# Weight sums of a Strassen product: two of four made by DMAs that add, all of them turned into additions

## The chip, the cores and the metric

The kernel runs on one core of a Trainium2 chip. A core has five engines with an instruction queue each: TensorE (PE), VectorE (DVE), ScalarE (ACT), GpSimd (POOL) and SyncE (SP), beside 16 DMA engines that all queues share. The metric is the device time of one execution in microseconds (us).

## The reference

One layer of a residual block on x of 512 tokens by 2048 features, in float32. What matters here is the second half, the feed-forward part with a hidden width of 8192:

```
h2 = rmsnorm(x, g_mlp)
u  = relu(h2 @ w_up)          # 2048 x 8192
x  = x + (u * u) @ w_down     # 8192 x 2048
return rmsnorm(x, g_final)
```

Before it come an input projection, two kinds of attention (8 heads each) and the output projection `w_out`.

## The kernel before

**Precision.** Every float32 operand of a matmul is split into a high part (a cast to fp32r on ACT, tiles `wh`, `wx`, `fh`) and a low part (value minus high part on DVE, tiles `wl`, `wx`, `fl`), by `split`, lines 60 and 61. `mm3` makes one product of three matmuls: high x high, high x low, low x high (lines 93 to 95). A matmul with `wl` therefore needs DVE's half, one with `wh` alone only ACT's.

**The first feed-forward product.** It is cut by Strassen's method in Winograd's form: of two 2 x 2 block matrices, seven products instead of eight, each on sums of blocks. The activations' seven forms `F[p]` (p = 1 to 7) are made once by `a_form`. The weights go through in 32 units of 256 columns. A unit has four blocks of 128 rows x 8 x 128 float32 (512 KB each): b11 and b12 in one loaded tile, b21 and b22 in another (`wu`, 1024 KB; five such tiles in the pool `rw`, so two and a half units are held; unit 0's b11 and b12 lie in tiles `wq`). Its seven products have 24 matmuls of 256 columns each, 8 steps of three. They need the weights in this form:

- p = 1: b11 itself; p = 5: b11 replaced by b12 - b11 (line 557)
- p = 6: b11 replaced by b22 - b11 (line 559); p = 2: b21; p = 3: b22
- p = 4: b21 replaced by b21 - b11 (line 561); p = 7: b12 replaced by b22 - b12 (line 563)

The sums are made in place by DVE. Each product takes a pair of tiles for the high and the low part from four pairs that go round in the order in which the program calls the products (`hi_lo`), so a product's split waits until PE has read the product four before it. That order is, for each unit: product 1 of the new unit, 4 of the old one, 5, 6 of the new, 3 of the old, 2 and 7 of the new. The results go to PSUM (`psa`, `psb`, `psc`), from there by ACT and DVE to `c`, and every two units are turned, seven forms at a time, into the left operand of the second product and stored to DRAM (`store_form`, tiles `st`, `ufd`).

**What sets the order.** The program is written in the order of these calls; a scheduler then fixes the order of each engine's instructions before the run, by costs of its own. At run time each queue goes strictly in its order and waits by semaphores.

**The start of this product.** The output projection ends with four additions of its result to x (line 487, DVE), 16 transposes on PE (line 496), the scaling on ACT (line 500) and the last quarter of the forms F. Unit 0's weights are split in the middle of it.

## Time and profile before

| | |
|---|---|
| time, median of 3 runs | 2093.42 us (2093.0 to 2095.84) |
| span of the profiled execution | 2090.6 us |
| own time of the profiled execution | not recorded apart from its span; the median of the runs is 2.8 us above the span |
| PE, DVE, ACT, POOL busy | 99%, 75%, 49%, 3% of the span |
| first feed-forward product | about 802 to 1470 us of the span |
| DMA queue of SP and POOL | 335.64 MB on SP's queue, none on POOL's |

Page and trace are of one execution. The span runs from the first to the last instruction; a busy share is the time an engine's instructions took, and instructions that only issue DMAs are not counted as busy. A row of a group names the line, the engine, the operation, out<-in by the program's names with buffer numbers left out, the count, the busy time in us and the mean in ns, and behind the second bar the idle time of the engine just before these instructions and what ended it. A row of waits gives who waited for whom: us in total, times, longest. A row of a stretch of time gives for each engine the busy us and the count, then the granted clock of PE, the share of the DMA engines in use, and GB/s.

### The profile page before, as it was taken

What the parts mean: (1) busy time and instruction counts of PE and PEld (TensorE: products, weight loads), DVE (VectorE), ACT (ScalarE), POOL (GpSimd) and SP (SyncE); (2) the same over time, 40 slices, a digit from 0 to 9 for tenths busy, and PEclk for the clock granted to TensorE, in tenths of its full rate; (3) what the DMA queues carried; (4) which work ended last, traced back from release to release, by engine and by line L of the source; (5) the groups of instructions that cost most, each with busy time, mean ns of one, the idle gap of its engine ahead of it and who ended that gap; (6) DMA issues with size and microseconds to landing.
All of it is one profiled execution on the core that took longest, in us unless ns stands there. A gap on an engine that the chain in (4) does not pass through costs nothing.

```text
span 2090.6 us, 29838 instructions
## 1 busy us (share of the span) xinstructions
PE 2070.1 (99%) x12084; PEld 1841.0 (88%) x12084; DVE 1570.7 (75%) x1744; ACT 1034.2 (49%) x1396; POOL 52.9 (3%) x76
## 2 busy tenths in 40 slices
PE   9999999999999999999999999999999999999998
PEld 8888888888898888999999999999888888888886
DVE  5454545665677567888888888888798988888886
ACT  6333334444445555556665666666744443333433
POOL 0000000010000000000000000000000000000003
PEclk9999999999999999999999999999999999999999
DMA  6323332323323444466566566567856664663732
GB/s 193 81 87 85 83 89 72 90 75 87 81 81 111 147 145 152 138 206 192 185 219 189 185 205 205 176 201 248 299 201 251 249 225 172 249 250 134 271 111 81
DMA packets 239930, 339.68 MB, mean 162 GB/s; under 512 B 7936, under 2 KB 154416, under 8 KB 233776
## 3 DMA queue, kind: packets, MB, share of 16 engines
q1 hardware_dynamic: 238832, 335.64, 48.9%
q8 instruction: 95, 1.56, 0.3%
q10 hardware_dynamic: 960, 2.13, 0.3%
q14 instruction: 43, 0.35, 0.0%
HBM read 272.20 MB, written 65.54 MB: 162 GB/s over the span
## 4 chain that ended last, share of the span: by engine, by line
PE 98%; DVE 1%; ACT 0%; issue 0%; DMA 0%; SPq 0%; ACTq 0%
PE accd L93 8%; PE accd L94 8%; PE accd L95 8%; PE psa L94 6%; PE psa L93 6%; PE psa L95 6%; PE accq L95 6%; PE accq L94 6%; PE accq L93 6%; PE psc L94 3%; PE psc L95 3%; PE psc L93 3%; PE acco L95 3%; PE acco L94 3%; PE acco L93 3%; PE accv L93 3%
## 5 line engine op out<-in xcount | busy, mean ns | idle before, releaser
L60 ACT CAST wh<-wu 128x1024 fp32r<-128x1024 f32 x164 | 170.9, 1048 | 134.8 <-PE psa L94 55.3
L61 DVE TENSOR_TENSOR wl<-wu,wh 128x1024 fp32r<-128x1024 f32 x164 | 199.4, 1221 | 45.0 <-ACT wh L60 44.7
L94 PE MATMUL psa<-fl,wh 128*128 128x256 f32 x776 | 219.8, 283 | 1.8 <-DVE fl L61 1.8
L93 PE MATMUL psa<-fh,wh 128*128 128x256 f32 x776 | 219.9, 283 | 0.5 <-ACT s L572 0.5
L95 PE MATMUL psa<-fh,wl 128*128 128x256 f32 x776 | 219.7, 283 | 0.0
L61 DVE TENSOR_TENSOR wl<-wraw,wh 128x1024 fp32r<-128x1024 f32 (+2 forms) x133 | 158.7, 1194 | 80.1 <-ACT wh L60 73.8
L60 ACT CAST wh<-wd 128x1024 fp32r<-128x1024 f32 (+1 forms) x136 | 134.6, 999 | 168.6 <-PE accd L95 107.5
L60 ACT CAST wh<-wraw 128x1024 fp32r<-128x1024 f32 (+2 forms) x133 | 135.4, 1019 | 156.5 <-PE accq L94 77.6
L95 PE MATMUL accq<-hH,wl 128*128 128x512 f32 x512 | 200.4, 391 | 0.0
L93 PE MATMUL accq<-hH,wh 128*128 128x512 f32 x512 | 200.1, 391 | 0.0
L94 PE MATMUL accq<-hL,wh 128*128 128x512 f32 x512 | 200.0, 391 | 0.0
L61 DVE TENSOR_TENSOR wl<-wd,wh 128x1024 fp32r<-128x1024 f32 (+1 forms) x136 | 155.5, 1153 | 41.9 <-ACT wh L60 41.4
L93 PE MATMUL accd<-wh,uf 128*128 128x512 f32 x436 | 169.7, 389 | 0.9 <-issue 0.9
L94 PE MATMUL accd<-wl,uf 128*128 128x512 f32 x436 | 169.6, 389 | 0.0
L95 PE MATMUL accd<-wh,uf 128*128 128x512 f32 x436 | 169.6, 389 | 0.0
L94 PEld LDWEIGHTS psa<-fl,wh 128*128 128x128 f32 x776 | 149.0, 192 | 2.2 <-DVE fl L61 2.2
L60 ACT CAST wx<-wd 128x1024 fp32r<-128x1024 f32 (+1 forms) x88 | 87.5, 1000 | 127.3 <-PE accd L95 75.9
L93 PEld LDWEIGHTS psa<-fh,wh 128*128 128x128 f32 x776 | 149.0, 192 | 1.0 <-ACT s L572 0.7
L95 PEld LDWEIGHTS psa<-fh,wl 128*128 128x128 f32 x776 | 149.0, 192 | 0.2 <-DVE wl L61 0.2
L61 DVE TENSOR_TENSOR wx<-wd,wx 128x1024 fp32r<-128x1024 f32 (+1 forms) x88 | 100.7, 1153 | 23.6 <-ACT wx L60 23.2
L94 PEld LDWEIGHTS accq<-hL,wh 128*128 128x128 f32 x512 | 96.2, 188 | 19.5
L95 PEld LDWEIGHTS accq<-hH,wl 128*128 128x128 f32 x512 | 96.1, 188 | 19.3
(300 smaller groups left out, 5491.9 us busy)
## 6 DMA issues: line engine op xcount, KB each, us to landing
wu<-in_w_up_dram SPq DMA_DIRECT2D x63, 1024.0 KB, 6.7
ufd<-st SPq DMA_DIRECT2D x98, 512.0 KB, 6.8
wd<-in_w_down_dram SPq DMA_DIRECT2D x48, 1024.0 KB, 6.1
wraw<-in_w_in_dram SPq DMA_DIRECT2D x84, 512.0 KB, 3.7
uf<-ufd SPq DMA_DIRECT2D x42, 1024.0 KB, 5.9
wraw<-in_w_out_dram SPq DMA_DIRECT2D x32, 512.0 KB, 3.6
wd<-in_w_down_dram SPq DMA_DIRECT2D x16, 768.0 KB, 6.2
uf<-ufd SPq DMA_DIRECT2D x14, 768.0 KB, 5.6
```

The lines of the kernel that those rows point to most:

```text
L60: ins = act.copy(hi, src)
L61: lows[0] = dve.tensor_tensor(lo, src, hi.bitcast(F32), op=ALU.subtract)
L93: pe.matmul(out, sh, mh, start=first, stop=False, skip_group_check=True)
L94: pe.matmul(out, sh, ml, start=False, stop=False, skip_group_check=True)
L95: pe.matmul(out, sl, mh, start=False, stop=last, skip_group_check=True)
```

## The change

The sums for p = 5 and p = 7 are made by DMAs that add their source to what lies at the destination: for p = 5 the block b12 is read a second time from DRAM and added to b11; for p = 7 b22 is added to b12 from on-chip memory to on-chip memory. Each sum is issued on POOL's queue in two halves of 256 KB, in runs of 512 bytes. Since they can only add, the signs change: p = 5 uses b12 + b11, p = 6 b22 + (b12 + b11), p = 4 b21 + b11, p = 7 b22 + b12. The forms of the activations and the last step of the results (`self.c`) take the opposite signs in return. Product 5 no longer reads b12, so b12 stays as loaded until p = 7.

```diff
-    def a_form(p, c, out, s=None):
+    def a_form(p, c, out, s=None, sums=False):
...
-            dve.tensor_tensor(s, a21, a22, op=ALU.add)
+            dve.tensor_tensor(s, a21, a22, op=ALU.subtract if sums else ALU.add)
...
-            dve.tensor_tensor(a12, a12, s, op=ALU.subtract)
+            dve.tensor_tensor(a12, a12, s, op=ALU.add if sums else ALU.subtract)
...
+    def add_dma(out, src):
+        for h in (slice(0, KC // 4), slice(KC // 4, KC // 2)):
+            pool.dma_start(out[:, h, :], src[:, h, :], accum_op=ALU.add)
...
+            self.w12 = rows_[0][:, :, (2 * u + 1) * P:2 * (u + 1) * P]
...
             if p == 5:
-                dve.tensor_tensor(b11, b12, b11, op=ALU.subtract)
+                add_dma(b11, self.w12)
             if p == 6:
-                dve.tensor_tensor(b11, b22, b11, op=ALU.subtract)
+                dve.tensor_tensor(b11, b22, b11, op=ALU.add)
             if p == 4:
-                dve.tensor_tensor(b21, b21, b11, op=ALU.subtract)
+                dve.tensor_tensor(b21, b21, b11, op=ALU.add)
             if p == 7:
-                dve.tensor_tensor(b12, b22, b12, op=ALU.subtract)
+                add_dma(b12, b22)
...
-                dve.tensor_tensor(self.c[:, 1, t2], self.m, self.C, op=ALU.add)
+                dve.tensor_tensor(self.c[:, 1, t2], self.C, self.m, op=ALU.subtract)
...
-                dve.tensor_tensor(self.c[:, 1, t1], self.m6, self.C, op=ALU.add)
+                dve.tensor_tensor(self.c[:, 1, t1], self.C, self.m6, op=ALU.subtract)
```

In the changed kernel the line of the adding DMAs is 533, of the sums for p = 6 and p = 4 it is 564 and 566, and of the evictions (before 578, 580, 584) 583, 585, 589. The scheduler also orders the queues anew.

**DVE at unit 10** (`wu_8904` and `wu_8906` before, `wu_8924` and `wu_8926` now, are its two weight tiles; `wu_8669`, `wu_8671` and `wu_8687`, `wu_8689` those of unit 9; a row of L61 that reads such a tile is the low half of a product's split, a row with `st` or of L458 to L464 belongs to `store_form`). Before, from product 1 of unit 10 to its product 5:

```order
L61 TENSOR_TENSOR wl_8912<-wu_8904,wh_8911 128x1024
L464 TENSOR_TENSOR c_8136<-c_8136 128x2x256
L61 TENSOR_TENSOR st_8941<-c_8136,st_8941 128x512
L584 TENSOR_TENSOR c_8603<-s6_8570,psc_8442 128x256
L557 TENSOR_TENSOR wu_8904<-wu_8904 128x8x128
L61 TENSOR_TENSOR wx_8947<-wu_8671,wx_8947 128x1024
L580 TENSOR_TENSOR c_8603<-s1_8703,psb_8674 128x256
L563 TENSOR_TENSOR wu_8904<-wu_8906,wu_8904 128x8x128
L61 TENSOR_TENSOR wl_8977<-wu_8904,wh_8976 128x1024
```

Now, the same stretch:

```order
L61 TENSOR_TENSOR wl_8932<-wu_8924,wh_8931 128x1024
L585 TENSOR_TENSOR c_8620<-s1_8721,psb_8692 128x256
L61 TENSOR_TENSOR wx_8967<-wu_8689,wx_8967 128x1024
L583 TENSOR_TENSOR c_8620<-psc_8693,s7_8921 128x256
L61 TENSOR_TENSOR wl_8998<-wu_8924,wh_8997 128x1024
```

The sums of lines 557 and 563 are gone, and between the two splits of unit 10 stand only two evictions and a split of unit 9. In unit 9 the scheduler put ten rows of `store_form` and others there.

**POOL.** Before, behind the last select of the attention stand only multiplications at the end of the kernel:

```order
L221 AFFINE_SELECT w_5014<-w_5014 128x3x128
L221 AFFINE_SELECT w_5014<-w_5014 128x128
L782 TENSOR_TENSOR m2_14223<-m2_14223,gf_18072 128x512 x4
L782 TENSOR_TENSOR m3_14281<-m3_14281,gf_18072 128x512 x4
L782 TENSOR_TENSOR m4_14339<-m4_14339,gf_18072 128x512 x2
```

Now 64 pairs of DMAs stand between them, here of units 7 to 10 (`<-in_w_up_dram` is the sum for p = 5, `<-wu` that for p = 7):

```order
L533 DMA wu_8215<-wu_8217 128x4x128 x2
L533 DMA wu_8215<-in_w_up_dram 128x4x128 x2
L533 DMA wu_8452<-wu_8454 128x4x128 x2
L533 DMA wu_8452<-in_w_up_dram 128x4x128 x2
L533 DMA wu_8687<-wu_8689 128x4x128 x2
L533 DMA wu_8924<-wu_8926 128x4x128 x2
L533 DMA wu_8687<-in_w_up_dram 128x4x128 x2
L533 DMA wu_8924<-in_w_up_dram 128x4x128 x2
```

As a rule a unit's p = 7 pair stands ahead of its p = 5 pair; in every fourth unit (5, 9, 13 and so on) the next unit's p = 7 pair stands ahead too.

**DVE at unit 0 and 1.** Before, the rows at the end of the output projection:

```order
L61 TENSOR_TENSOR wl_6657<-wq_6647,wh_6656 128x1024
L557 TENSOR_TENSOR wq_6647<-wq_6648,wq_6647 128x1024
L61 TENSOR_TENSOR wl_6688<-wq_6647,wh_6687 128x1024
L487 TENSOR_TENSOR x2_6212<-x2_6212,acco_6208 128x512
L487 TENSOR_TENSOR x2_6212<-x2_6212,acco_6209 128x512
```

Now:

```order
L61 TENSOR_TENSOR wl_6657<-wq_6647,wh_6656 128x1024
L487 TENSOR_TENSOR x2_6212<-x2_6212,acco_6208 128x512
L61 TENSOR_TENSOR wl_6689<-wq_6647,wh_6688 128x1024
L487 TENSOR_TENSOR x2_6212<-x2_6212,acco_6209 128x512
L487 TENSOR_TENSOR x2_6212<-x2_6212,acco_6210 128x512
L487 TENSOR_TENSOR x2_6212<-x2_6212,acco_6211 128x512
```

The third row is the split of unit 0's product 5, ahead of three of the four additions. A little later the split of unit 1's product 1 (fourth row) stands behind the eviction of unit 0's product 2:

```order
L566 TENSOR_TENSOR wu_6651<-wu_6651,wq_6647 128x8x128
L61 TENSOR_TENSOR fl3_5085<-hr_6522,fh3_5084 128x512
L585 TENSOR_TENSOR c_6759<-s1_6684,psb_6654 128x256
L61 TENSOR_TENSOR wx_6829<-wu_6822,wx_6829 128x1024
L61 TENSOR_TENSOR wl_6792<-wq_6648,wh_6791 128x1024
```

That eviction stood ahead of it before too; but on PE, 6 matmuls of product 6 and the whole of product 7 of unit 0 came between the end of product 2 and unit 1's product 1. Now 5 matmuls of product 6 do, and product 7 follows unit 1's product 1 (so the last two rows have changed places on DVE).

**PE** has the same matmuls in another order of products. In a group of four units, written p(unit), with `a|b` where two are interleaved, it is now: 7(7), 1(8), 4(7), 5(8)|3(7), 2(8)|6(8), 7(8), 1(9), 4(8), 3(8), 5(9), 6(9)|2(9), 1(10)|7(9), 4(9), 5(10), 2(10)|6(10), 3(9), 1(11)|7(10), 4(10), 5(11), 6(11), 3(10), 2(11), 7(11). Before, every unit had 1, 4 (old), 5, 6, 3 (old), 2, 7 with an exchange of a few matmuls between neighbours. In numbers of matmuls: from the end of 6(9) to the start of 5(10) stand 22 of 2(9), 2 of 1(10), 24 of 7(9), 22 of 1(10) and 24 of 4(9), together 94.

## The prediction

> **What bounds the kernel now.** I read the page first (busy time, the chain of work that ended last), then the engines by stage, then PE's waits, then the rows of single instructions around one weight unit.

> ```profile
> PE 2070.1 (99%) x12084; PEld 1841.0 (88%) x12084; DVE 1570.7 (75%) x1744; ACT 1034.2 (49%) x1396; POOL 52.9 (3%) x76
> PE 98%; DVE 1%; ACT 0%; issue 0%; DMA 0%; SPq 0%; ACTq 0%
> core 0: us, PE busy (x) PEld busy (x) DVE busy (x) ACT busy (x) POOL busy (x), PEclk, DMA share, GB/s
> 400.00:690.00 290.00, 290.00 (x1473) 248.17 (x1473) 190.66 (x227) 140.14 (x181) 19.76 (x30) 1.00 0.31 91
> 802.00:860.00 58.00, 54.33 (x404) 51.30 (x403) 44.58 (x52) 30.95 (x48) 0.00 (x0) 1.00 0.46 146
> 860.00:1409.00 549.00, 549.00 (x4578) 549.00 (x4577) 470.24 (x532) 335.46 (x449) 0.00 (x0) 1.00 0.62 194
> ```

> PE carries the chain. The change lies in the first feed-forward product (about 802 to 1470 us of the span), and in its steady part, 860 to 1409, PE is busy in every microsecond at a clock of 1.00 while DVE is at 86% (470.24 of 549). 549 us over 4578 matmuls is 0.12 us each; one product of 24 takes 2.88 us and a unit of seven 20.2 us. The only idle time of PE in this product lies at its start, 58.00 - 54.33 = 3.7 us:

> ```profile
> PE psa L94 <- DVE fl L61: 1.8, 2, 0.9
> PE psb L93 <- ACT wh L60: 1.3, 1, 1.3
> PE psa L93 <- ACT s L572: 0.5, 1, 0.5
> ```

> So work taken off DVE can win 3.7 us at most. Anything that makes a weight arrive late costs PE directly. A clear gain would need over 0.2% (4.2 us; below that a measurement of this kernel cannot tell a change from none, and my chances are cut there).

> **What is removed.** Of the four sums of a unit, two leave DVE.

> ```profile
> L557 DVE TENSOR_TENSOR wu<-wu 128x1024 f32<-128x1024 f32 x27 | 32.9, 1220 | 0.2
> L563 DVE TENSOR_TENSOR wu<-wu 128x1024 f32<-128x1024 f32 x27 | 32.8, 1216 | 0.0
> L60 ACT CAST wh<-wu x164: 1029/1048/1057, 820.9 to 1455.6; 128x1024 fp32r<-128x1024 f32 x164
> L61 DVE TENSOR_TENSOR wl<-wu,wh x164: 1212/1219/1227, 823.8 to 1456.7; 128x1024 fp32r<-128x1024 f32 x164
> ```

> 64 sums of 1.22 us are 78 us of DVE, all beside a busy PE but one: at the start L563 stands ahead of the low halves (fl) that PE waits for. I count its 1.2 us as won: -1.2. Subtractions that become additions, and the four edits of signs, keep engine, count and shape: 0. The two sums left (p = 6 and p = 4) stay on DVE.

> **What is added: 128 DMAs on POOL's queue, 256 KB each**, in 512 B runs, two to a sum. The p = 7 sum (b12 += b22) needs only the loaded weights, now that p = 5 no longer reads b12, and is used last in its unit: it has most of a unit and costs 0, except where it stands ahead of something on POOL (below). The p = 5 sum is the critical one. It may not start before the low half of product 1 has been read from b11, and product 5's high half (1.05 us of ACT) waits for it. How much time is there? In one unit of the trace of before (low half of product 1, then the sum, then product 5's low half; last, PE's products 7 and 1 and the first matmul of product 5):

> ```profile
> 1249.37 1.23 DVE L61 TENSOR_TENSOR wl<-wu,wh 128x1024 fp32r<-128x1024 f32 x1 [0.50 <-ACT wh L60]
> 1252.63 1.22 DVE L557 TENSOR_TENSOR wu<-wu 128x1024 f32<-128x1024 f32 x1
> 1256.37 1.21 DVE L61 TENSOR_TENSOR wl<-wu,wh 128x1024 fp32r<-128x1024 f32 x1
> 1253.92 0.28 PE L93 MATMUL psa<-fh,wh 128*128 128x256 f32 x1
> 1259.68 0.28 PE L93 MATMUL psc<-fh,wh 128*128 128x256 f32 x1
> ```

> 1259.68 - (1249.37 + 1.23) - 1.05 = 8.0 us. The new order gives the same by counting. The four pairs of weight buffers go round in program order, so product 1 of a unit is split when PE ends product 6 of the unit before. Call the time from the end of product 1's low half to the landing of the sum c; the room for c is:

> - Units 4k+2 and 4k+3 (14 of them from unit 4 on): PE has 94 matmuls between that end and product 5, 11.3 us; less 1.05 + 1.22 for product 1's split and 1.05 for the cast: 8.0 us.
> - Units 4k+1 (7): PE has been given one product more, but on POOL the next unit's p = 7 pair stands ahead of this unit's p = 5 pair, and its weights are loaded only after product 7 of the unit before has been split. Product 5 starts 166 matmuls (19.9 us) after the end of product 5 of the unit before; used up are a split (2.3), a load (6.8), the two issues of the p = 7 pair (2.6, at the 1.3 us each found below) and the cast (1.05): room 7.2 us.
> - Units 4k (7): 118 matmuls, 14.2 us: room 10.8 us. Units 2 and 3 have five products: 11.1.
> - Unit 1: product 1 is now split only after the eviction of unit 0's product 2 on DVE (0.42 + 1.22), which PE follows with 5 matmuls of its own: 0.8 us of PE lost, and two products later product 5 is due: room 4.5 us.
> - Unit 0: its p = 5 split stands on DVE ahead of three of the four residual additions (L487), for which the transposes and all of F wait:

> ```profile
> 802.79 1.23 DVE L61 TENSOR_TENSOR wl<-wq,wh 128x1024 fp32r<-128x1024 f32 x1 [0.26 <-ACT wh L60]
> 807.99 1.23 DVE L61 TENSOR_TENSOR wl<-wq,wh 128x1024 fp32r<-128x1024 f32 x1 [2.70 <-ACT wh L60]
> 812.30 0.69 DVE L487 TENSOR_TENSOR x<-x,acco 128x512 f32<-128x512 f32 x1 [0.68 <-PE acco L95]
> 812.10 1.91 PE L496 MATMUL tr<-ident,x 128*128 128x128 f32 x16
> ```

> Today these end at 813.0. Then: 804.0 + c, 2.3 for the split, 1.9 for three additions, that is 808.2 + c: room 4.8 us, and PE has only transposes there.

> **How long is c?** Before has no DMA that adds and none from POOL, so I bound it. Transfers of this size, first in the projection of queries (0.31 of the DMA engines busy, also 512 B runs), then in the changed stage (0.62 busy); then what an issue takes on SP, and a POOL instruction on two operands:

> ```profile
> wraw<-in_w_in_dram SPq DMA_DIRECT2D x30, 512.0 KB, 3.7
> wu<-in_w_up_dram SPq DMA_DIRECT2D x56, 1024.0 KB, 6.8
> ufd<-st SPq DMA_DIRECT2D x87, 512.0 KB, 6.7
> ufd<-st SPq DMA_DIRECT2D x14, 256.0 KB, 6.4
> L593 SPq DMA_DIRECT2D ufd<-st x98: 512/514/1416, 874.2 to 1462.7; - x98
> L782 POOL TENSOR_TENSOR m<-m,gf 128x512 f32<-128x512 f32 x15 | 19.2, 1304 | 1432.5 <-ACT junk L780 1432.5
> ```

> Low end: the whole sum as one light load, 3.7 us. High end: two transfers of this stage one after the other, 13.4 us. Between them I take the row of the same stage and size, 6.4 us from issue (0.5 of it) to landing, 0.4 more for reading the old value (1024 KB instead of 256 cost 0.4), and two issues of g each: c = 6.4 - 0.5 + 0.4 + 2g = 6.3 + 2g. With SP's g of 0.5 it is 7.3. [...]

> [...]

> **The sum at c = 8.9.** Unit 0: 8.9 - 4.8 = 4.1. Unit 1: 0.8 + 8.9 - 4.5 = 5.2. DVE's relief: -1.2. Units 4k+2 and 4k+3: 14 x 0.9 = 12.6. Units 4k+1: 7 x 1.7 = 11.9. Units 4k: 0. Together +32.6 us on a span of 2090.6. The span of this profile is 2.8 us under the median of the runs, 2093.4, which I keep: 2093.4 + 32.6 = 2126. None of it comes back later, because behind this product PE's order is the old one and PE is full.

> New waits, and who stands behind them: ACT's cast of product 5 waits for the second DMA, and in its queue wait the casts of products 6 and 2 and the copies that empty PSUM; that is why a late sum reaches PE within a product or two. SP's weight loads now also wait for the adds into the buffer that they overwrite, but the splits they waited for before come after those adds: 0.

> **Rivals.**
> - *The sums land in time (no change).* The total at small c is (c - 4.8) + (0.8 + c - 4.5) - 1.2 = 2c - 9.7 (0.8 - 1.2 below the rooms), within 4.2 us for c up to 6.9 us; g is then small too, and units 4k+1 have room enough. For it: the 3.7 us row, and DMA engines idle 38% of the time. Against it: every row of this stage is at 6.4 or more. Time 2093 to 2098; at c = 6.0, 2096. [...]
> - *The DMA engines fill up (much slower).* 12.5 us of a unit's 20.2 are in use (0.62). A unit's adds move 1.05 MB; at 91 / 0.31 = 294 GB/s for all engines that is 3.6 us (share 0.80) if an add costs what a copy does, 7.1 us (0.97) with two reads. At 0.97 each transfer queues, c goes to the high end, 13.4: 17.1 + 14 x 5.4 + 7 x 6.2 + 7 x 2.6 = 154 us, 2248. From 7.7 us of adds a unit the engines themselves set the pace. [...]
> - *Faster.* DVE's two instructions fewer at the start take away all 3.7 us and c is under 4.5: 2089.7 at best, still inside 0.2%. It needs something the profile does not show.

> **Chances.** c between 6.9 and 11.3: 0.55, time 2098 to 2185 (at 11.3: 12.9 + 14 x 3.3 + 7 x 4.1 + 7 x 0.5 = 91 us). c above that, with full engines: 0.15. In time: 0.27. Faster: 0.03. So slower 0.70, same 0.27, faster 0.03; the likeliest is 2126. The range 2091 to 2190 leaves out most of the full-engine case.

> **What the profile after would show.** Right: PE waits in this stage on ACT's cast or DVE's low half of p = 5 (wh or wl from wu), those in turn on POOL's DMAs, some 1 to 2 us in three units of four, 4 to 5 us each at units 0 and 1; DVE 78 us shorter; DMA share 0.75 to 0.85; landing of the adding DMAs 6 to 9 us. Wrong: no PE wait after 860 us (c under 8), or a DMA share over 0.95, loads of wu landing in 10 us and more, and waits in every unit.

## The result and the profile after

The changed kernel takes 2426.0 us (median of 4 runs, 2424.5 to 2429.9) against 2093.7 us before: a ratio of 1.159, 95% interval 1.157 to 1.161. It is 332 us slower, where I had forecast 33. The profiled execution has a span of 2424.2 us, 333.6 more than the one of before.

The page of the changed kernel: busy time of PE, POOL's DMA queue, the chain that ended last and two lines of DMA issues.

```profile
PE 2147.3 (89%) x12084; PEld 1903.3 (79%) x12084; DVE 1504.3 (62%) x1680; ACT 1029.6 (42%) x1396; POOL 219.2 (9%) x204
q0 software_dynamic: 67584, 33.56, 11.2%
PE 69%; issue 11%; DMA 9%; DVE 6%; ACT 3%; POOL 2%; SPq 0%; ACTq 0%; DVEq 0%; POOLq 0%
wu<-wu POOLq DMA_DIRECT2D x62, 256.0 KB, 3.9
wu<-in_w_up_dram POOLq DMA_DIRECT2D x62, 256.0 KB, 5.1
```

POOL's busy time rises from 52.9 to 219.2 us, which is 128 issues of 1.30 us: the instructions by which POOL issues a DMA do count as busy here. PE executes the same 12084 matmuls, but is busy 77.2 us longer, and 256.4 us of the span more than before it is not busy. Both have to be explained. The chain, all PE before, now has 9% DMA and 11% "issue", time in which an engine waited for nothing that the profile shows. The stretch 860 to 1409 us, where PE had been busy in every microsecond at a clock of 1.00 (columns as there):

```profile
860.00:1409.00 549.00, 414.09 (x3079) 405.73 (x3079) 272.70 (x314) 221.16 (x299) 93.51 (x72) 0.84 0.68 159
```

1499 matmuls fewer are done in it, the clock is 0.84, and the DMA engines stand at 0.68 only. Four rows of the waits (us in total, times, longest):

```profile
ACT wh L60 <- DMA wu<-in_w_up_dram: 255.3, 23, 16.2
PE psc L93 <- ACT wh L60: 202.4, 24, 15.2
PE psc L93 <- ACT wx L60: 30.1, 7, 6.2
PE tr L496 <- DVE x L487: 5.6, 1, 5.6
```

This is the path that the prediction named: the p = 5 sum arrives late, ACT's cast waits for it, PE's product 5 (`psc`) waits for the cast. One group of four units on PE, the first matmul of product 5 in units 4k+1, 4k+2, 4k+3 and 4k (start, us; in brackets the wait):

```profile
1346.48 0.58 PE L93 MATMUL psc<-fh,wh 128*128 128x256 f32 x1 [14.84 <-ACT wh L60]
1372.71 0.58 PE L93 MATMUL psc<-fh,wh 128*128 128x256 f32 x1 [5.93 <-ACT wh L60]
1400.13 0.58 PE L93 MATMUL psc<-fh,wx 128*128 128x256 f32 x1 [3.76 <-ACT wx L60]
1431.83 0.58 PE L93 MATMUL psc<-fh,wh 128*128 128x256 f32 x1 [8.09 <-ACT wh L60]
```

Every unit waits, and the pattern repeats. POOL's queue in the first of these units shows why (`wu<-wu` is the next unit's p = 7 pair, then come the two halves of p = 5):

```profile
1321.33 1.30 POOL L533 DMA_DIRECT2D wu<-wu  x1 [10.57 <-DMA wu<-in_w_up_dram]
1326.48 1.29 POOL L533 DMA_DIRECT2D wu<-wu  x1 [3.84 <-issue]
1331.78 1.31 POOL L533 DMA_DIRECT2D wu<-in_w_up_dram  x1 [4.02 <-issue]
1340.52 1.30 POOL L533 DMA_DIRECT2D wu<-in_w_up_dram  x1 [7.42 <-issue]
```

ACT's cast that waits for the sum, in the same unit:

```profile
1345.38 1.04 ACT L60 CAST wh<-wu 128x1024 fp32r<-128x1024 f32 x1 [16.21 <-DMA wu<-in_w_up_dram]
```

An issue takes POOL 1.30 us, as predicted, but behind it POOL stands 3.8 to 7.4 us before the next one: "issue", no semaphore. By the trace these four adds land 4.8, 5.0, 8.4 and 4.8 us after their issues start, and each next issue starts 0.3 us after the landing before it. So the four adds go out one at a time. They also differ in length. In a unit 4k, the two halves of the p = 5 sum from issue to landing:

```profile
1414.52:1425.57 11.05, 9.21 (x77) 9.01 (x76) 2.50 (x4) 3.27 (x5) 1.31 (x1) 1.00 0.84 231
1425.88:1430.65 4.77, 0.00 (x0) 0.00 (x0) 0.00 (x0) 0.00 (x0) 1.30 (x1) 0.60 0.46 55
```

The first half meets transfers of SP's queue (DMA share 0.84 at 231 GB/s) and takes 11.1 us, the second is alone (0.46 at 55) and takes 4.8. The other loss is in the clock. Windows around one wait of 3.81 us, which ends at 1274.89 (the columns end with the granted clock, the DMA share and GB/s):

```profile
1270.00:1271.08 1.08, 1.08 (x10) 0.88 (x8) 0.00 (x0) 0.00 (x0) 0.00 (x0) 1.00 1.01 269
1274.89:1276.30 1.41, 0.94 (x3) 0.65 (x3) 1.41 (x2) 1.01 (x3) 0.43 (x1) 0.50 0.33 42
1277.70:1279.10 1.40, 1.40 (x9) 1.40 (x9) 1.33 (x2) 0.64 (x1) 0.86 (x1) 0.50 0.44 171
1280.60:1282.00 1.40, 1.40 (x14) 1.40 (x13) 1.40 (x3) 1.40 (x3) 0.00 (x0) 1.00 1.07 132
```

PE comes back at a clock of 0.50 and stays there for some 5 us, most of product 5. 30 waits of PE in this stage end in a matmul of 0.58 us (0.28 at full clock); 77.2 / 30 = 2.6 us lost behind each.

### The profile page after: what moved, and what is told of

It is laid out like the page before. It is cut to its first block, busy times and chain, and to the rows that moved or that the text cites. A ratio compares the mean times of both kernels' runs of the same rounds, so it can differ in the third digit from the quotient of the medians.

```text
span 2424.2 us, 30113 instructions
## 1 busy us (share of the span) xinstructions
PE 2147.3 (89%) x12084; PEld 1903.3 (79%) x12084; DVE 1504.3 (62%) x1680; ACT 1029.6 (42%) x1396; POOL 219.2 (9%) x204
## 3 DMA queue, kind: packets, MB, share of 16 engines
q0 software_dynamic: 67584, 33.56, 11.2%
## 4 chain that ended last, share of the span: by engine, by line
PE 69%; issue 11%; DMA 9%; DVE 6%; ACT 3%; POOL 2%; SPq 0%; ACTq 0%; DVEq 0%; POOLq 0%
DMA wu<-in_w_up_dram 7%; PE accd L93 7%; PE accd L95 7%; PE accd L94 7%; PE accq L95 5%; PE accq L94 5%; PE accq L93 5%; DVE wl L61 2%; PE accv L93 2%; PE accv L95 2%; PE acco L93 2%; PE accv L94 2%; PE acco L94 2%; PE acco L95 2%; PE psc L95 2%
## 5 line engine op out<-in xcount | busy, mean ns | idle before, releaser
L61 DVE TENSOR_TENSOR wl<-wu,wh 128x1024 fp32r<-128x1024 f32 x164 | 197.0, 1222 | 333.9 <-ACT wh L60 333.4
L60 ACT CAST wh<-wu 128x1024 fp32r<-128x1024 f32 x164 | 167.4, 1046 | 395.3 <-DMA wu<-in_w_up_dram 255.3
L93 PE MATMUL psc<-fh,wh 128*128 128x256 f32 x376 | 130.7, 347 | 203.2 <-ACT wh L60 202.4
L93 PEld LDWEIGHTS psc<-fh,wh 128*128 128x128 f32 x376 | 92.0, 245 | 209.8 <-ACT wh L60 209.8
L93 PE MATMUL psa<-fh,wh 128*128 128x256 f32 x776 | 220.7, 285 | 4.1 <-ACT s L577 4.1
L94 PE MATMUL psa<-fl,wh 128*128 128x256 f32 x776 | 220.2, 284 | 0.0
L95 PE MATMUL psa<-fh,wl 128*128 128x256 f32 x776 | 218.6, 285 | 0.0
L61 DVE TENSOR_TENSOR wl<-wraw,wh 128x1024 fp32r<-128x1024 f32 (+2 forms) x133 | 158.9, 1196 | 78.5 <-ACT wh L60 72.1
L60 ACT CAST wh<-wd 128x1024 fp32r<-128x1024 f32 (+1 forms) x136 | 134.4, 999 | 166.3 <-PE accd L95 106.3
L60 ACT CAST wh<-wraw 128x1024 fp32r<-128x1024 f32 (+2 forms) x133 | 135.4, 1019 | 154.9 <-PE accq L94 77.6
L95 PE MATMUL accq<-hH,wl 128*128 128x512 f32 x512 | 200.4, 391 | 0.0
L93 PE MATMUL accq<-hH,wh 128*128 128x512 f32 x512 | 200.1, 391 | 0.0
L94 PE MATMUL accq<-hL,wh 128*128 128x512 f32 x512 | 200.0, 391 | 0.0
L61 DVE TENSOR_TENSOR wl<-wd,wh 128x1024 fp32r<-128x1024 f32 (+1 forms) x136 | 155.5, 1154 | 38.1 <-ACT wh L60 37.6
L93 PE MATMUL accd<-wh,uf 128*128 128x512 f32 x436 | 169.7, 389 | 1.0 <-issue 1.0
L95 PE MATMUL accd<-wh,uf 128*128 128x512 f32 x436 | 169.6, 389 | 0.0
L94 PE MATMUL accd<-wl,uf 128*128 128x512 f32 x436 | 169.6, 389 | 0.0
L93 PEld LDWEIGHTS psa<-fh,wh 128*128 128x128 f32 x776 | 150.4, 194 | 4.3 <-ACT s L577 4.3
L94 PEld LDWEIGHTS psa<-fl,wh 128*128 128x128 f32 x776 | 150.2, 194 | 0.0
L95 PEld LDWEIGHTS psa<-fh,wl 128*128 128x128 f32 x776 | 149.1, 193 | 0.0
L60 ACT CAST wx<-wd 128x1024 fp32r<-128x1024 f32 (+1 forms) x88 | 87.5, 999 | 129.3 <-PE accd L95 73.7
L95 PE MATMUL psc<-fh,wl 128*128 128x256 f32 x376 | 125.4, 333 | 7.0 <-DVE wl L61 7.0
## 6 DMA issues: line engine op xcount, KB each, us to landing
wu<-in_w_up_dram SPq DMA_DIRECT2D x63, 1024.0 KB, 7.0
ufd<-st SPq DMA_DIRECT2D x98, 512.0 KB, 5.0
wd<-in_w_down_dram SPq DMA_DIRECT2D x48, 1024.0 KB, 6.1
wraw<-in_w_in_dram SPq DMA_DIRECT2D x84, 512.0 KB, 3.8
uf<-ufd SPq DMA_DIRECT2D x42, 1024.0 KB, 6.0
wraw<-in_w_out_dram SPq DMA_DIRECT2D x32, 512.0 KB, 3.5
wu<-wu POOLq DMA_DIRECT2D x62, 256.0 KB, 3.9
wu<-in_w_up_dram POOLq DMA_DIRECT2D x62, 256.0 KB, 5.1
```

The costliest lines, as they stand in the source:

```text
L60: ins = act.copy(hi, src)
L61: lows[0] = dve.tensor_tensor(lo, src, hi.bitcast(F32), op=ALU.subtract)
L93: pe.matmul(out, sh, mh, start=first, stop=False, skip_group_check=True)
L94: pe.matmul(out, sh, ml, start=False, stop=False, skip_group_check=True)
L95: pe.matmul(out, sl, mh, start=False, stop=last, skip_group_check=True)
```

## The experiments

My theory after the result: the program's setting `dynamic_dma_scratch_size` (2048 in the changed kernel; I call it the room, in the expectations room for descriptors, though no trace shows descriptors) lets one adding DMA of 256 KB out at a time, so a second waits until the first has landed; and PE pays for a wait twice, with the wait and with a slow restart. Rivals: the new form of the sums itself (order, signs); the place of the p = 7 pair on POOL's queue; DMA engines that are full; something in POOL's queue that no room would change. All experiments are edits of the changed kernel, timed against the kernel before.

**1 and 2. No adds by DMA; only p = 7 by DMA.**

```
 if p == 5:
-    add_dma(b11, self.w12)
+    dve.tensor_tensor(b11, b12, b11, op=ALU.add)
 if p == 7:                                # first run only
-    add_dma(b12, b22)
+    dve.tensor_tensor(b12, b22, b12, op=ALU.add)
```

> All four sums on DVE again, but in the new form (additions, the order of products and the four changed signs kept); no DMA adds. My theory (the adding DMAs are issued one at a time, so the p = 5 sum lands some 12 to 15 us after the low half of product 1, and PE then also restarts at half pace): all of the loss goes, 2090 to 2098 us, PE at clock 1.00 from 860 to 1409. Rival (the new form itself, that is the order of the sums and what waits for what, costs the time): near 2426, or at least 50 us above 2093.

> Only the p = 7 sum is made by DMAs (two of 256 KB a unit), p = 5 is on DVE. My theory: the p = 7 pair takes some 9 to 11 us even one at a time and has most of a unit (20.2 us): no wait of PE in the steady part, 2090 to 2098 us. Rival (the DMA engines fill up, or an add slows the loads of the weights, so that either pair costs): the DMA share stays near 0.7, loads of wu land later than 7 us, and the time is above 2150.

Measured: 2093.5 us, ratio 1.0000 (0.9992 to 1.0009), and 2092.1 us, ratio 0.9994 (0.9986 to 1.0003). The new form costs nothing, and the p = 7 pair alone costs nothing. With that pair alone, 860 to 1409 us:

```profile
860.00:1409.00 549.00, 548.69 (x4571) 548.38 (x4570) 440.66 (x503) 330.39 (x448) 69.87 (x54) 1.00 0.82 220
```

PE is full again with the DMA engines at 0.82, a higher share than in the changed kernel. So the mean share does not tell whether a sum comes late.

**3. Only p = 5 by DMA** (the second of the two edits above alone).

> Only the p = 5 sum is made by DMAs, p = 7 is on DVE. My theory (one adding DMA in flight): the second half is still issued some 5 us after the first, c = 5.0 + 5.1 to 5.9 = 10.1 to 10.9 us (time from the end of product 1's low half to the landing); PE waits 2 to 3 us in half of the units and longer at units 0 and 1: 2140 to 2190 us, the upper end if each of these waits also brings the half clock. Rival (it was the p = 7 pair standing ahead on POOL's queue that made p = 5 late): the halves are issued 1.3 us apart, c = 8 to 9, 2100 to 2126 us.

Measured: 2364.3 us, ratio 1.131 (1.129 to 1.133). 271 of the 332 us come from this pair, with nothing ahead of it on POOL. Two of its rows on POOL:

```profile
1262.20 1.29 POOL L533 DMA_DIRECT2D wu<-in_w_up_dram  x1 [20.48 <-DVE c L589]
1271.53 1.30 POOL L533 DMA_DIRECT2D wu<-in_w_up_dram  x1 [8.03 <-issue]
```

Issues in one pair are 4.9 to 10.8 us apart, and c, from the first issue to the cast, is 9.8 to 15.7 us. So the queue is held up as I said, but c was larger than I expected (I had taken the quiet gap of 5 us for all units), and so was the time.

**4 and 8. The room raised from 2048 to 2560, and its control.** In both, two padding tiles are taken out and a third is cut; the control keeps 2048.

```
-nc = _bacc.Bacc(..., dynamic_dma_scratch_size=2048)
+nc = _bacc.Bacc(..., dynamic_dma_scratch_size=2560)   # not in the control
 ...
-cp.tile([P, 96], F32, name="pad0")        # and pad1; pad2 from 120 to 104 columns
```

> [...] If the room for descriptors is what keeps the halves apart: the second half is issued right behind the first (1.3 us apart), c falls to 9 us, and the time to 2126 to 2200 us. Rival (POOL takes one adding DMA at a time whatever the room): issues stay 4 to 5 us apart and the time stays at 2426, within 10 us.

> Control for the larger room: the same padding tiles taken away as there, the room for descriptors left at 2048 bytes. All theories of the room expect the time of the changed kernel, 2426 within 15 us, with the second half 4 to 5 us or more behind the first. Rival (what counted there was where the buffers lie): near the 2291 of the run with the larger room.

Measured: 2290.8 us, ratio 1.0945 (1.0919 to 1.0971), and for the control 2431.3 us, ratio 1.162 (1.160 to 1.164). POOL's rows with more room:

```profile
1245.94 2.60 POOL L533 DMA_DIRECT2D wu<-wu  x2 [14.71 <-DMA wu<-in_w_up_dram]
1250.48 1.30 POOL L533 DMA_DIRECT2D wu<-in_w_up_dram  x1 [1.94 <-DVE c L462]
1255.18 1.31 POOL L533 DMA_DIRECT2D wu<-in_w_up_dram  x1 [3.41 <-issue]
1280.48 2.60 POOL L533 DMA_DIRECT2D wu<-in_w_up_dram  x2 [23.99 <-DVE wl L61]
```

Two halves now go out in one row (x2, 2.60 us). Where the p = 7 pair goes first, the p = 5 halves have to wait again: their cast starts 16.5 us after the first p = 5 issue, and PE waits 10.8 us. It was the room, and 135 us of the loss went with it. But 197 us were left, above the 2126 to 2200 us that I expected. The room was not all.

**5. Plain copies in place of the adds** (`accum_op=ALU.add` left out).

> The changed kernel with plain copies in place of the adding DMAs, same sizes, same queue, same order; the additions of p = 5 and p = 7 are left out. [...]

This kernel leaves the two sums out: b11 and b12 are overwritten. Measured: 2148.9 us, ratio 1.027 (1.025 to 1.028), 56 us above before and inside the 2095 to 2200 us that I expected. Halves go out back to back, at 0.75 us each instead of 1.30. What POOL's queue took of the 16 DMA engines (packets, MB, share of the span):

```profile
q0 software_dynamic: 10240, 33.56, 4.2%
```

4.2% of 2147.0 us over 128 DMAs is 0.70 us of all engines for 256 KB; the adds of the changed kernel take 11.2% of 2424.2 us, that is 2.12 us, three times as much. The copies also have far fewer packets (80 a DMA against 528), so this run alone does not say whether the second source or the short pieces cost the time.

**6. Each sum in four DMAs of 128 KB, room as it was** (the loop in `add_dma` takes four slices of 2).

> [...] Rival (POOL's queue holds few DMAs whatever their size, and the gain of the larger room came from elsewhere): one or two at a time, four in a row take 4 x 4 = 16 us or more, and the time is above 2430.

Measured: 2323.9 us, ratio 1.110 (1.108 to 1.112).

```profile
1236.52 3.70 POOL L533 DMA_DIRECT2D wu<-in_w_up_dram  x3 [11.81 <-DVE c L589]
1244.77 1.22 POOL L533 DMA_DIRECT2D wu<-in_w_up_dram  x1 [4.55 <-issue]
```

Three go out together and the fourth waits: here it starts 0.3 us after the first add has landed. (Where the first lands in 3.0 us, four go out without a gap.) So with the room at 2048 three adds of 128 KB are out at once, or one of 256 KB, and at 2560 two of 256 KB (run 4). I had counted on three, by an estimate of my own of what an add needs; no trace shows that need. The time is slightly above the 2150 to 2320 us that I expected; one reason can be that an issue hardly gets shorter with half the bytes (1.22 us against 1.30), so four cost POOL 4.9 us.

**7 and 10. Only p = 5 by DMA with the room at 2560; the same, reading b12 from SBUF** (`add_dma(b11, b12)`).

> [...] My theory: both halves in flight and nothing ahead of them: c = 2 x 1.3 + 5.5 to 7.8 = 8.1 to 10.4 us, waits of 0 to 2.4 us in the units, which bring little or no half clock: 2100 to 2170 us. Rival (the loads of the weights on the DMA engines make the add late, not the queue): c stays at 11 us or more as in the run with p = 5 alone, and the time above 2250.

> [...] Theory (in the few us of the add the DMA engines are full, and an add holds them 2.1 us per 256 KB whatever it reads): the same engine time per add, c 6.5 to 12 as there, 2200 to 2265 us. Rival (reading the weights a second time from DRAM is what makes it land late): c falls by 2 us or more, 2095 to 2170 us.

Measured: 2240.1 us, ratio 1.070 (1.068 to 1.072), and 2233.2 us, ratio 1.067 (1.065 to 1.068). So it is not the second read from DRAM. Both halves are in flight and nothing is ahead, and still 147 us are lost. The windows from the first issue to the cast, four units of the first of these runs:

```profile
1277.32:1283.80 6.48, 6.48 (x57) 6.48 (x56) 5.11 (x7) 4.41 (x7) 2.61 (x2) 1.00 0.85 147
1299.27:1311.34 12.07, 8.62 (x72) 8.42 (x71) 3.74 (x5) 3.27 (x6) 2.62 (x2) 1.00 0.93 231
1328.22:1337.86 9.64, 6.88 (x58) 6.67 (x56) 6.13 (x9) 2.32 (x5) 2.61 (x2) 1.00 0.92 220
1352.27:1361.29 9.02, 8.35 (x70) 8.14 (x68) 2.71 (x4) 0.75 (x2) 2.62 (x2) 1.00 0.91 201
```

c is 6.5, 12.1, 9.6 and 9.0 us (first number behind the window), and the DMA share in just these windows is 0.85 to 0.93, while the mean over 860 to 1409 us is 0.67. In these four the add lands the later, the more is moved meanwhile (147 to 231 GB/s, last column). Where c is 9 us, PE waits under 2 us for the cast; yet that is not free:

```profile
1263.04 0.39 PE L93 MATMUL psc<-fh,wh 128*128 128x256 f32 x1 [1.62 <-ACT wh L60]
```

The stretch of 3.41 us that holds this wait, and windows from its end on:

```profile
1261.74:1265.15 3.41, 1.35 (x9) 1.15 (x10) 2.10 (x2) 2.26 (x3) 0.00 (x0) 1.00 0.00 0
1266.00:1267.50 1.50, 1.50 (x9) 1.50 (x9) 1.50 (x2) 1.50 (x2) 0.00 (x0) 0.50 0.00 0
1269.00:1271.00 2.00, 2.00 (x19) 2.00 (x18) 2.00 (x2) 0.63 (x1) 0.00 (x0) 1.00 0.00 0
```

After the wait of 1.62 us PE starts at full clock, waits 0.76 us more for DVE's low half, and falls to 0.50 some 2 us after its restart, for 3.41 us. In run 4 the same two waits (1.68 us, ending at 970.87, and 0.76 us) leave the clock at 1.00:

```profile
967.80:971.22 3.42, 1.74 (x14) 1.48 (x12) 0.38 (x1) 1.45 (x3) 2.54 (x2) 1.00 0.68 82
971.22:974.63 3.41, 2.65 (x23) 2.51 (x22) 3.38 (x4) 2.35 (x4) 0.06 (x1) 1.00 1.07 121
974.00:978.00 4.00, 4.00 (x36) 4.00 (x35) 4.00 (x5) 2.31 (x3) 0.00 (x0) 1.00 0.10 13
```

The difference is where the waits fall. In the changed kernel's trace all 32 stretches at 0.50 of this product last 3.41 us or a multiple of it, up to 17.07 us. In run 7 both waits lie almost wholly in one such step, and PE is busy for 1.35 us of it; in run 4 they lie in two, with 1.74 and 2.65 us. Counted in this way in the traces of the changed kernel and the twelve runs whose clock fell in this product: behind 276 steps it fell, with PE busy for at most 0.57 of the step, and behind 1953 it stayed, with at least 0.46; in the changed kernel's trace alone it fell behind 32 steps, with at most 0.43, and stayed behind 169, with at least 0.48. So a wait of 1.6 us can cost the clock or not, by where it falls.

The time, too, is above the 2100 to 2170 us that I expected. The rival of run 7 (the traffic makes the add late, not the queue alone) is half right: c fell, but not by enough.

**11, 12 and 15. Long runs.** The four parts of a unit's weights one behind the other in SBUF, loaded in two transfers of 512 KB in place of one of 1024 KB, so that an add has runs of 2 KB; p = 5 reads b12 from SBUF; room as it was. Run 12 is the control with all sums on DVE; run 15 has one DMA of 512 KB a sum, with runs of 4 KB.

```
-raw = rw.tile([P, KC // 2, 2 * P], F32, tag="rw", name="wu")
-sp.dma_start(raw, rows_[i][:, :, cols])
-self.b.append([raw[:, :, j * P:(j + 1) * P] for j in range(2)])
+raw = rw.tile([P, 2, KC // 2, P], F32, tag="rw", name="wu")
+for j in range(2):
+    sp.dma_start(raw[:, j], rows_[i][:, :, (2 * u + j) * P:(2 * u + j + 1) * P])
+self.b.append([raw[:, j] for j in range(2)])
```

> [...] Theory A (an add pays per run of 512 B, in engine time and in descriptors): engine time per add falls from 2.1 to about 0.7 us per 256 KB, halves go out back to back, c 5 to 7 us, 2093 to 2130 us. Theory B (an add pays per byte, since it reads two sources): engine time stays at 1.4 to 2.1 us and the time above 2200.

> Control for the run before: the same layout and loads of 512 KB, all four sums on DVE, no adding DMA. 2090 to 2100 us by every theory; more would mean that the layout or the loads cost by themselves.

> As the run with runs of 2 KB, but each sum in one adding DMA of 512 KB with runs of 4 KB. Measured so far for 256 KB: 2.12 us of all 16 engines with 512 runs of 512 B, 1.49 with 128 runs of 2 KB, 0.70 for a plain copy. My theory (an add pays per byte, about 1.28 us for 256 KB, and 1.6 ns per run on top): with 64 runs 1.39 us for 256 KB, 2.77 a sum; two issues a unit fewer on POOL; PE still waits in some units: 2110 to 2165 us. Rival (it pays per run alone, and the share left at 2 KB is queueing): below 1.0 us for 256 KB, and 2095 to 2110 us.

Measured: 2172.5 us, ratio 1.0375 (1.035 to 1.040); control 2094.0 us, 1.0002 (0.9992 to 1.0011); one DMA a sum 2144.8 us, 1.025 (1.024 to 1.027). POOL's queue in run 11:

```profile
q0 software_dynamic: 18432, 33.56, 8.8%
```

And in run 15:

```profile
q0 software_dynamic: 9216, 33.56, 8.1%
```

8.8% of 2167.8 us is 1.49 us of all engines for 256 KB, 8.1% of 2141.2 us is 1.36 (1.39 expected). So an add pays for both: about 1.3 us for the bytes, and 1.6 ns for each run (an estimate from the three). Theory A of run 11 was wrong on the size (0.7) and on the time (2093 to 2130), theory B on the time; run 15 came out as expected. Against the plain copy of run 5 an add holds the engines 1.36 / 0.70 = 1.9 times as long with runs of 4 KB, and 3.0 times with runs of 512 B. Of the 332 us, 52 are left in run 15, about as many as with plain copies of 512 B runs (56, run 5).

**9, 13 and 14. What a late sum costs PE.** Run 9 is run 3 with 24 matmuls more a unit in front of product 5; runs 13 and 14 have no adding DMA, but make the p = 5 sum late on POOL:

```
 if p == 5:                                # run 9
     add_dma(b11, self.w12)
+    for a in range(3 * KC // 2):
+        w_ = F[1][0][:, a % (KC // 2), :]
+        pe.matmul(self.C, w_[:, :P], w_, start=a == 0, stop=a == 3 * KC // 2 - 1, ...)
 if p == 5:                                # runs 13 and 14: 6 and 8 times
-    add_dma(b11, self.w12)
+    pool.tensor_tensor(b11, b12, b11, op=ALU.add)
+    for i in range(6):
+        pool.tensor_tensor(b11[:, :4], b11[:, :4], b12[:, :4], op=ALU.add if i % 2 else ALU.subtract)
```

> The kernel with p = 5 alone by DMAs (2364 us), and 24 matmuls more a unit (2.88 us at full clock) that need nothing and whose result product 5 overwrites; they stand in front of product 5, most of them right in front of it, so that PE works for 2.88 us of its wait there. My theory (a wait of over some 3.5 us lets the granted clock fall, and the product behind it then runs at half pace, some 2.5 to 2.9 us more): waits of 3.7 to 7.9 us become 0.8 to 5, in about 20 of 31 units the half pace goes, 20 x 2.7 = 54 us won, against 3 or 4 units without a wait that pay 2.88: 2310 to 2335 us, faster with more work. Rival (the half pace does not come from PE standing idle): no gain, 2364 or up to 31 x 2.88 = 89 us more, 2453.

> No DMA that adds: p = 7 on DVE, p = 5 added by POOL itself (128x1024), followed by six POOL instructions on half of it (three subtractions and three additions of b12, so the sum stays), to make the sum late by a known time: c = 2.6 + 6 x 1.3 = 10.4 us by POOL's 1.3 us for 512 columns. My theory (a late sum costs its overrun, and the half pace only where PE waits over some 3.5 us): about 15 units with a room of 7.2 to 8.0 wait 2.4 to 3.2 us at full clock, the others nothing, units 0 and 1 some 6 each: 40 to 65 us, 2135 to 2160. Rival (every wait of PE brings the half pace): 15 x 2.7 = 40 us more, 2175 to 2200.

> The same with eight POOL instructions on a half instead of six: c = 13.0 us, about what the changed kernel's sums took, with the DMA engines as in the kernel before. Overruns alone: 15 x 5.4 in the units with less room, 15 x 2.2 in the others, 8 and 9 at units 0 and 1, that is 131 us, 2225. My theory adds the half pace (2.5 to 2.9 us) to the 17 waits over 3.5 us: 45 us more, 2250 to 2290 us, with matmuls at 0.24 us start to start behind these waits and a granted clock of 0.50. Rival (a wait costs what it lasts; in the changed kernel the low clock came with the DMA traffic): 2205 to 2235 us at a clock of 1.00.

Measured: run 9, 2369.7 us, ratio 1.132 (1.130 to 1.135), 5 us more than run 3. The wait was not filled but moved: PE now waits for the copy of another tile, which stands behind the same cast on ACT.

```profile
PE psa L93 <- ACT s L580: 102.6, 22, 6.1
```

92 us of added matmuls (768 x 0.12) cost 5 us, and my 2310 to 2335 us were missed. PE is busy 70.5 us longer than in run 3 (2219.0 against 2148.5), not 92, and idle some 62 us less: part of the added work ran in idle time, and about 22 us of slow running went. 18 waits still end in a matmul of 0.58 us (29 in run 3). That fits a price of some 2 us for a slow restart, but the waits moved too, so the run does not measure it.

Runs 13 and 14: 2352.8 us, ratio 1.124 (1.122 to 1.126), and 2420.1 us, ratio 1.156 (1.154 to 1.158), far above both of my ranges. The sum was later than meant (in run 14 one add and eight halves take 2.4 + 13.9 = 16.3 us in the rows below, not 13), and DVE got slower beside a computing POOL. The same subtraction, in the run with all sums on DVE (busy time, mean ns of one):

```profile
L61 DVE TENSOR_TENSOR st<-c,st 128x512 fp32r<-128x512 f32 x105 | 69.6, 686 | 20.0 <-ACT st L60 19.9
```

And in run 13:

```profile
L61 DVE TENSOR_TENSOR st<-c,st 128x512 fp32r<-128x512 f32 x105 | 117.4, 1146 | 7.0 <-ACT st L60 6.2
```

Of the 105 in run 13, the 53 that had no POOL instruction beside them took 684 ns on average, the 32 that ran wholly beside one 1947 ns. So these runs are no clean price of a delay. POOL's rows of one unit of run 14:

```profile
1256.57 2.41 POOL L562 TENSOR_TENSOR wu<-wu 128x1024 f32<-128x1024 f32 x1 [11.52 <-DVE wl L61]
1259.05 13.93 POOL L564 TENSOR_TENSOR wu<-wu 128x512 f32<-128x512 f32 x8
```

What these runs do show is the clock. Windows behind a wait of 11 us of PE, which ends at 1276.56, in a stage whose DMA share is 0.39:

```profile
1276.56:1279.00 2.44, 1.19 (x4) 0.90 (x5) 2.41 (x3) 0.00 (x0) 0.00 (x0) 0.50 0.91 348
1279.00:1281.50 2.50, 2.50 (x13) 2.50 (x13) 1.39 (x2) 1.66 (x2) 0.00 (x0) 0.50 0.01 3
1283.00:1285.00 2.00, 2.00 (x18) 2.00 (x17) 1.66 (x3) 1.05 (x1) 0.00 (x0) 0.91 0.26 57
```

The clock stands at 0.50 with a DMA share of 0.01, in a kernel without adding DMAs. The slow restart needs neither them nor their traffic; the rival that tied it to them is out.

## Why the prediction was wrong, step by step

Right were the direction, the path (p = 5 sum, cast, product 5), that DVE's relief is worth nothing, that p = 7 is hidden where it is alone (run 2), and POOL's 1.3 us an issue. That last one was luck: no run of before has an issue on POOL, and the 1.3 in c = 6.3 + 2 x 1.3 = 8.9 is a multiplication there; the changed kernel's issues take 1.30 us, those of runs 5 and 11 0.75 and 0.86. The step that failed is the choice of c. I had both ends, 3.7 us and "two transfers one after the other", 13.4 us, and took 8.9 because I let the halves overlap: nothing in the program made the second wait, so I issued it 1.3 us behind the first. In the trace it goes out 4.9 to 11.9 us behind, 0.3 us after the first has landed, and c is 9.9 to 16.6 us. The rows below compare my sum, the same formula at the high end, and the waits of PE over 0.9 us with the slower PE beside them (322 of the 333.6 us; the rest are shorter waits).

| us | as predicted, c = 8.9 | the same formula at c = 13.4 | measured |
|---|---|---|---|
| units 0 to 3 | 9.3 | 18.3 | 26.5 waits |
| units 4k+2, 4k+3 | 12.6 | 75.6 | 63.4 waits (14) |
| units 4k+1 | 11.9 | 43.4 | 102.1 waits (7) |
| units 4k | 0 | 18.2 | 53.3 waits (7) |
| DVE's relief | -1.2 | -1.2 | not seen |
| slower PE | 0 | 0 | 77.2 |
| together | 32.6 | 154.3 | 322.5 |

By my own rooms the formula also leaves out 2.3 us each for units 2 and 3 at c = 13.4.

- Units 4k+1: I charged the p = 7 pair ahead with its two issues, 2.6 us. One at a time it takes 1331.78 - 1321.33 = 10.5 us, 7.9 more. 1.7 of overrun, 7.9, and c = 13.6 (1345.38 - 1331.78) instead of 8.9, that is 4.7 more: 14.3 us; the waits are 14.2 to 15.2.
- Units 4k+2 and 4k+3: the room of 8.0 us was right within half a microsecond: c of 11.3 and 13.5 in the group shown against waits of 3.76 and 5.93.
- Units 4k: the room of 10.8 us, which I had counted in matmuls from PE's order, was 8.1 (c of 16.2 less the wait of 8.09). That count left DVE's order out. In the trace product 1's low half starts 2.4 to 2.8 us after its cast has ended, because DVE first makes product 7's low half (`wx`) and two rows of `store_form`. In unit 12 (product 1's cast, DVE's `wx`, product 1's low half):

```profile
1161.35 1.04 ACT L60 CAST wh<-wu 128x1024 fp32r<-128x1024 f32 x1
1162.82 1.22 DVE L61 TENSOR_TENSOR wx<-wu,wx 128x1024 fp32r<-128x1024 f32 x1
1165.16 1.22 DVE L61 TENSOR_TENSOR wl<-wu,wh 128x1024 fp32r<-128x1024 f32 x1
```

- The price of a wait: I took the overrun alone and a clock of 1.00. The 77.2 us are a term that my sum does not have. In the changed kernel's trace the granted clock fell to 0.50 behind steps of 3.41 us in which PE was busy for at most 0.43 of the time. Such a step need not be idle: in run 7 the clock fell behind one in which PE was busy for 1.35 us. The half pace lasts 3 to 6 us behind a wait here.
- Full DMA engines, the rival with 0.15: I bounded the adds at 3.6 to 7.1 us a unit. They take 4 x 2.12 = 8.5, above the 7.7 at which I said that the engines set the pace. This shows most where the queue no longer holds the adds back (runs 4 and 7). In the changed kernel the mean share is 0.68, with one add out at a time; but the rival has a part there too, in the first half of a pair, which takes 11.1 us at a share of 0.84 in the unit shown above. I had said that this rival would show as a share over 0.95; the waits in every unit that I had named with it came without that.
- Landing: medians of 3.9 and 5.1 us from issue, below the 6 to 9 that I had said. They hide two cases. From unit 4 on, one half of a p = 5 sum meets little else and lands in 4.6 to 5.0 us; the other meets transfers of SP's queue and lands in 6.2 to 11.6 us (the longest in units 4k). DVE is 66 us shorter, not 78.

What is not settled: how much of the last 52 us of run 15 is the adds' own time and how much the traffic that they meet. Plain copies lose 56 us in run 5, so a good part of it may need no add at all; that is not shown.

## What to carry to other kernels

Ask how many DMAs from POOL can be out at once before letting two overlap in a forecast: with the room of this program at 2048 it was one add of 256 KB in 512 B runs, at 2560 two. "issue" behind a POOL DMA is how the lack showed (3.8 to 7.4 us in the unit shown). Judge a critical transfer by the DMA share in its own microseconds, not by the stage's mean: the same stage had PE full at 0.82 (run 2) and late sums at 0.68 (changed kernel). Count the room for a late operand in the queues of all engines that it passes, not in PE's alone: DVE's order took 2.4 to 2.8 us of it in the units 4k. And where PE is the bound, a wait can cost more than its length: in the changed kernel some 2.6 us of half clock on top, while waits under 2 us brought it in some places and not in others.
